# Two-layer hybrid encoder on one core: zero-padded score products, a corrected planning clock, a hand-written beginning, and one run of products with v per branch

## The chip, the core and the metric

The kernel runs on one core of a Trainium2 chip. A core has TensorE (matrix products, PE in the profile), VectorE (DVE), ScalarE (ACT), GpSimd (POOL) and SyncE (SP, which here only issues transfers), each with its own queue of instructions that it takes in order, and 16 DMA engines that move data between HBM and the core's memory. Products are written to PSUM, eight banks of 128 partitions by 512 fp32. The metric is the device time of one execution in microseconds; lower is better.

## What is computed

Two layers of an encoder on 256 tokens of width 1024. Cut to what matters:

```python
h = rms_norm(x, norm_mix_g); proj = h @ w_in                        # 9 blocks of 256 columns
ret  = retention(rq, rk, rv) ...    # 4 heads of 64: (q k^T * decay) v
na   = softmax(q k^T / 8 + bias) v  # 4 heads of 64, 256 tokens
mo   = softmax(q mk^T / 8) mv       # 4 heads of 64, 256 memory tokens
pool = window means of pv, a 64x64 map per group
up = einsum('bsnc,ncd->bsnd', stack([ret, pool, na, mo]), w_branch)
x = x + (sigmoid(h @ w_gate) * up).sum(n) @ w_out
a, g = split(rms_norm(x, norm_ffn_g) @ w_ffn_in); x = x + (silu(a) * g) @ w_ffn_out
```

All weights are fp32, 151 MB of them are read once.

## The kernel before

**Main products.** The 256 tokens are two tiles (t = 0, 1) of 128. The weights come as 276 slots of 128x1024 in the order in which they are used. A slot is loaded by SP into one of 4 buffers `raw`, copied by ACT to `whi` (rounded to fp32r, `split_hi`), and DVE writes the remainder `wlo = raw - whi` (`split_lo`). The activations are split the same way (`hhi`/`hlo` after a norm, `bhi`/`blo` after a branch), and a product of 128 tokens with 512 columns is three instructions on PE: hi by whi, hi by wlo, lo by whi (`emit`). There are 3312 of them, 96 of which are 256 columns wide, the rest 512.

**Small work.** Norms, head norms, transposes, scores, softmax, the products with v and the rest are generators ("chains") that run between the main products. `to_heads` turns q and k to heads with the tokens in the free dimension: `LS` holds the hi part of a head on 64 partitions and the lo part on the other 64, `RS` the hi part of the other operand on both halves. `scores` makes the scores of a head for 128 tokens in two products of 256 columns: LS (128 partitions) by RS, and the 64 partitions of the hi part in LS by `RL`, the lo part of the other operand. `attention` is called for branch 2 (neighbourhood) and branch 3 (memory), and works on two heads at a time (r = 0, 1): scores into the banks B, maximum, exp, scaling into `SC`, transposes back to B, a copy to `PT`, products with v into C[1]. The retention in `branch_chain` does the same with decays `DD` in place of a softmax.

**Order.** The program is written out instruction by instruction. What decides the order is a planning clock (`Clock`): each instruction that is given out is entered with an assumed cost, and a chain goes on when, by that clock, its operands should be there (`soon`, `there`, `need`, `background`). `pump` decides by the same clock when the next slot is split, and `ready` which tile's slot PE takes next. The clock has no part in the execution on the chip: there each engine runs its queue in order and waits on semaphores.

**Beginning.** x comes in four transfers of 128x512, all on SP's queue in turn with the identity (with the gains, `ident_gain`) and the first weight slots. `half_norm` turns and splits each half tile; products of zeros fill PE until the first operands are there.

Since a helper records every instruction for the clock, all instructions have the same line (L59); they are told apart by the names of their tiles: `A`, `B`, `C` are PSUM banks, `sc` and `pt` the softmax tiles, `qk` the values v (in the retention too), `w` scratch, `mem` the retention's decays.

Of the kernel before, what the change touches and what calls it, by code (L numbers as in the profile page):

```python
# [15 lines left out]
P = 128  # L16
D = 1024
KD = D // P
S = 256
# [16 lines left out]
WARM = 6.6  # L36
WINDOW = (6, 4, 1.5, 0.4)
# [5 lines left out]
class Engine:  # L43
    """An engine of nc whose instructions are also entered in the clock."""
# [4 lines left out]
    def __getattr__(self, op):  # L49
        f = getattr(self.real, op)  # L50

        def call(*args, **kw):
# [5 lines left out]
            self.clock.enter(self.name, op, outs, [v for v in ins + rest if isinstance(v, bass.AP)], kw)  # L58
# [5 lines left out]
class Clock:  # L64
    """An estimate in microseconds of when each engine gets to what has been given to it:
    the small work is handed out when its operands should be there, so that no queue waits on it."""
# [3 lines left out]
    def __init__(self):  # L70
        self.at = dict.fromkeys(("PE", "ACT", "DVE", "POOL", "SP", "DMA"), 0.6)
        self.reads, self.writes = {}, {}
        self.mark = 0.0
        self.column = None

# [4 lines left out]
    def cost(self, eng, op, outs, ins, kw):  # L80
        n = max([x.free_size() for x in outs[-1:] + ins[:1]])
        if eng == "PE":
            o = outs[0]
            n = o.free_size() * (2 if self.now < WARM else 1)
            if op == "transpose":
                return n * 0.84e-3
            if ins[0].dtype == F32R:
                return n * 0.416e-3 + 0.003
# [5 lines left out]
            return max(n, 128) * 1.67e-3  # L94
        if eng == "ACT":
            return 0.1 + n * 0.83e-3 + 0.1 * (kw.get("accum_out") is not None) + 0.04 * isinstance(kw.get("scale"), bass.AP)
        if eng == "POOL":
            return 0.3 + 0.17 * n
        if op in ("tensor_copy", "tensor_scalar", "tensor_scalar_mul", "tensor_scalar_add", "memset"):
            return 0.07 + n * 0.55e-3  # L100
        return 0.07 + n * 1.05e-3 + 0.05 * (op == "scalar_tensor_tensor")
# [18 lines left out]
    def enter(self, eng, op, outs, ins, kw):  # L120
# [5 lines left out]
                + [max(self.last(self.writes, x, skip), self.last(self.reads, x, skip)) + self.LATENCY for x in outs] + [self.at[eng]])  # L126
        if op == "dma_start":
            self.at[eng] = t + 0.48
            t = max(self.at["DMA"], t + 1.1) + (outs + ins)[0].nbytes() / 360e3
            self.at["DMA"] = t  # L130
            end = t + 0.9
# [16 lines left out]
def tile_encoder(ctx: ExitStack, tc: tile.TileContext, a: dict, out: bass.AP):  # L148
# [29 lines left out]
    RL = st([P, 2, S], F32R, "rl")  # L178
# [73 lines left out]
    state = {"dma": 0, "hi": 0, "lo": 0, "free": 0, "urgent": 0}  # L252
# [7 lines left out]
    def issue_dmas(n=NR):  # L260
        while state["dma"] < min(n_slots, state["lo"] + n):
# [3 lines left out]
            if len(dims) == 2:  # L265
# [6 lines left out]
    def split_hi():  # L272
        j = state["hi"]
        nc.scalar.copy(WHI[j % NS], RAW[j % NR])
        state["hi"] += 1
# [11 lines left out]
    def pump():  # L287
        """split weights when the engines have caught up, the sooner the fewer slots are ready"""
# [43 lines left out]
    def start(gen, *reads):  # L332
        """reads: PSUM banks that gen still reads, until it calls done()"""
# [3 lines left out]
    def until(step):  # L337
        """a chain goes on after what it has just given out (None), that much later (a number), or at a time"""
        return step[0] if isinstance(step, tuple) else clock.mark + (step or 0)

    def background():
        """let every chain go on whose last instructions should be through"""
# [39 lines left out]
    def scale_rows(out, in_, col):  # L382
        """out = in_ * col, on the engine that is free sooner"""
# [6 lines left out]
    def hi_lo(hi, lo, ps, bank, flag):  # L390
        """hi now, lo when hi is there, which ends the hold on bank"""
# [14 lines left out]
    def half_norm(src, t, c, act, gain, flag, bank, pre=None):  # L406
        """Half c of src (token-major) transposed, times gain (there a column), and split.
        What follows the products with it scales by one over the RMS (rms_chain)."""
# [22 lines left out]
    def rms_chain(src, rs, junk, flag, after=()):  # L431
        """rs = one over the RMS of each row of src"""
# [11 lines left out]
    def norm(t, flag, gain, rs, pre):  # L444
        """both halves of the norm of X[t]"""
# [7 lines left out]
    def head_norm(ps, dst, g, scale=None):  # L453
        """dst = ps (times scale, by row) scaled to unit RMS in groups of 64, g of them."""
# [662 lines left out]
```

## Time and profile before

| | before |
|---|---|
| time, median of 3 runs | 851.39 us (849.38 to 854.74) |
| profiled execution, first to last instruction | 850.4 us |
| PE busy | 840.0 us (99%) |
| DVE busy | 553.3 us (65%) |
| ACT busy | 469.6 us (55%) |
| POOL busy | 28.6 us (3%) |
| moved by DMA | 152.86 MB, 180 GB/s in the mean |

Busy time of PE overlaps: a product's own duration is longer than the step from one product to the next, so a PE that is shown as busy may still have waited some tenths of a microsecond. The step from one start to the next is what has to be read. In the rows below, times are in microseconds from the start of the span.

### The profile page before, as it was taken

To read this page: it belongs to the slowest core of one execution; us is meant where nothing else is said; L and a number is where in the kernel's file an instruction comes from. 1 tells how busy PE (TensorE), PEld (TensorE's weight loads), DVE (VectorE), ACT (ScalarE), POOL (GpSimd) and SP (SyncE) were. 2 spreads that over 40 slices of the span, in tenths; PEclk is the share of its full clock that TensorE was granted. 3 is DMA by queue.
4 is the path that set the end of the run, shared out by engine and by line. 5 is a ranking of instruction groups with operands and counts; after the bars stand their busy time and mean duration, and the time that the engine had idled before them with its cause. 6 is when DMAs were issued, how large, how long until landed. Compare 5 with 4: busy or idle time off the path is not lost.

```text
span 850.4 us, 10796 instructions
## 1 busy us (share of the span) xinstructions
PE 840.0 (99%) x3934; PEld 678.6 (80%) x3934; DVE 553.3 (65%) x807; ACT 469.6 (55%) x722; POOL 28.6 (3%) x30
## 2 busy tenths in 40 slices
PE   8999999999999999999999999999999999999998
PEld 7887777778887888888888877777788878888886
DVE  5898776665667656555568778567665775665541
ACT  7867867444556444444469676664454654444430
POOL 0300100000000000000012001000000000000000
PEclk9999999999999999999999999999999999999999
DMA  8946764454558666665363567345554675656611
GB/s 267 315 131 202 246 201 132 131 191 160 191 169 259 188 196 187 186 188 186 96 218 121 173 216 250 134 124 182 165 170 131 190 252 183 190 181 192 193 53 50
DMA packets 103749, 152.86 MB, mean 180 GB/s; under 512 B 6416, under 2 KB 55312, under 8 KB 103696
## 3 DMA queue, kind: packets, MB, share of 16 engines
q1 hardware_dynamic: 103696, 152.17, 56.3%
q8 instruction: 31, 0.51, 0.2%
q14 instruction: 22, 0.18, 0.1%
HBM read 151.10 MB, written 1.05 MB: 179 GB/s over the span
## 4 chain that ended last, share of the span: by engine, by line
PE 94%; DMA 3%; DVE 1%; ACT 1%; SPq 0%; issue 0%; DVEq 0%; ACTq 0%
PE A L59 62%; PE B L59 27%; PE C L59 5%; DMA raw<-in_w_ffn_out 2%; DMA mem<-in_pool_a 1%; DVE wlo L59 1%; DMA x<-in_x 1%; ACT whi L59 1%; DVE w L59 0%; SPq L59 0%; DVE x L59 0%; DVEq L1113 0%; ACTq L59 0%
## 5 line engine op out<-in xcount | busy, mean ns | idle before, releaser
L59 DVE TENSOR_TENSOR wlo<-raw,whi 128x1024 fp32r<-128x1024 f32 (+1 forms) x275 | 329.9, 1211 | 183.6 <-ACT whi L59 182.7
L59 ACT CAST whi<-raw 128x1024 fp32r<-128x1024 f32 x272 | 284.3, 1051 | 221.2 <-PE A L59 102.1
L59 PE MATMUL A<-whi,hhi 128*128 128x512 f32 (+1 forms) x544 | 215.6, 396 | 0.1
L59 PE MATMUL A<-whi,hlo 128*128 128x512 f32 (+1 forms) x544 | 209.4, 385 | 0.0
L59 PE MATMUL A<-wlo,hhi 128*128 128x512 f32 (+1 forms) x544 | 209.0, 384 | 0.0
L59 PEld LDWEIGHTS A<-whi,hhi 128*128 128x128 f32 x544 | 102.4, 188 | 24.1 <-issue 5.5
L59 PEld LDWEIGHTS A<-whi,hlo 128*128 128x128 f32 x544 | 102.4, 188 | 21.2 <-DVE hlo L59 0.5
L59 PEld LDWEIGHTS A<-wlo,hhi 128*128 128x128 f32 x544 | 102.6, 189 | 17.9
L59 PE MATMUL B<-whi,hlo 128*128 128x512 f32 x288 | 112.3, 390 | 0.1
L59 PE MATMUL B<-whi,hhi 128*128 128x512 f32 x288 | 112.3, 390 | 0.0
L59 PE MATMUL B<-wlo,hhi 128*128 128x512 f32 x288 | 112.1, 389 | 0.0
L59 PE MATMUL A<-whi,bhi 128*128 128x512 f32 x272 | 109.2, 401 | 0.0
L59 PE MATMUL A<-whi,blo 128*128 128x512 f32 x272 | 106.3, 391 | 0.0
L59 PE MATMUL A<-wlo,bhi 128*128 128x512 f32 x272 | 106.1, 390 | 0.0
L59 PEld LDWEIGHTS B<-whi,hlo 128*128 128x128 f32 x288 | 54.0, 188 | 12.1 <-DVE hlo L59 0.9
L59 PEld LDWEIGHTS B<-wlo,hhi 128*128 128x128 f32 x288 | 54.1, 188 | 11.2
L59 PEld LDWEIGHTS B<-whi,hhi 128*128 128x128 f32 x288 | 54.1, 188 | 11.1
L59 PEld LDWEIGHTS A<-whi,bhi 128*128 128x128 f32 x272 | 51.1, 188 | 11.4 <-issue 0.8
L59 PEld LDWEIGHTS A<-whi,blo 128*128 128x128 f32 x272 | 51.0, 188 | 11.0
L59 PEld LDWEIGHTS A<-wlo,bhi 128*128 128x128 f32 x272 | 51.2, 188 | 9.7
L59 DVE SCALAR_TENSOR_TENSOR w<-B,rms,w 128x256 f32<-128x256 f32 x72 | 34.6, 482 | 3.9 <-ACT w L59 2.6
L59 ACT CAST bhi<-C 128x512 fp32r<-128x512 f32 x28 | 16.4, 587 | 35.2 <-PE C L59 35.1
(112 smaller groups left out, 614.9 us busy)
## 6 DMA issues: line engine op xcount, KB each, us to landing
raw<-in_w_ffn_in SPq DMA_DIRECT2D x176, 256.0 KB, 3.3
raw<-in_w_gate SPq DMA_DIRECT2D x64, 512.0 KB, 3.8
raw<-in_w_ffn_out SPq DMA_DIRECT2D x44, 512.0 KB, 4.0
raw<-in_w_in SPq DMA_DIRECT2D x36, 512.0 KB, 4.6
raw<-in_w_branch SPq DMA_DIRECT2D x16, 512.0 KB, 5.0
raw<-in_w_out SPq DMA_DIRECT2D x16, 512.0 KB, 4.1
raw<-in_w_mem_kv SPq DMA_DIRECT2D x8, 512.0 KB, 5.1
xn<-in_bias SPq DMA_DIRECT2D x4, 512.0 KB, 5.8
```

Of the source, the lines that this page charges most:

```text
L59: return f(*args, **kw)
```

## The change

Four things are changed, and comments and descriptions are taken out.

1. `RL` gets a second half per head, so that it has the lo part of a head on the head's own 64 partitions and zeros (written once by GpSimd) on the other 64. The second product of `scores` now contracts over all 128 partitions.
2. In `attention` and in the retention the products with v of all four heads stand in one run behind the second pair of heads, in place of one run behind each pair. The second pair's turned probabilities go to `SC`, which the transposes have been read from, so that `PT` stays with the first pair.
3. The planning clock's prices are changed: a 512-wide product from 0.216 to 0.227 us, DVE and DMA by some per cent, 0.2 us where PE goes from a 64-partition fp32 product to another kind or back, and 1.28 us where ACT goes from exp to sigmoid or back.
4. The work up to slot 2 is written out in `begin` rather than planned: x's tile 0 is turned in two quarters, then the first slot's products for tile 0, then tile 1. The identity and tile 1's first half are loaded on ACT's queue, slot 0 in two transfers, copied and subtracted in halves. At the end each second store of a half block goes on ACT's queue.

```diff
...
 WARM = 6.6
+TABLE_LOAD = 1.28
...
                 outs.append(rest.pop(0))
-            self.clock.enter(self.name, op, outs, [v for v in ins + rest if isinstance(v, bass.AP)], kw)
+            func = next((v for v in rest if isinstance(v, AF)), None)
+            self.clock.enter(self.name, op, outs, [v for v in ins + rest if isinstance(v, bass.AP)], kw, func)
...
         self.column = None
+        self.narrow = False
+        self.table = None
...
             n = o.free_size() * (2 if self.now < WARM else 1)
+            narrow = op == "matmul" and ins[0].dtype == F32 and o.partition_size() == HD
+            change = 0.2 * (narrow != self.narrow)
+            self.narrow = narrow
             if op == "transpose":
-                return n * 0.84e-3
+                return n * 0.845e-3 + change
             if ins[0].dtype == F32R:
-                return n * 0.416e-3 + 0.003
+                return n * 0.4167e-3 + 0.0135 + change
...
                     return 0.02
-            return max(n, 128) * 1.67e-3
+            return max(n, 128) * 1.67e-3 + change
...
         if eng == "POOL":
+            if op == "memset":
+                return 0.1 + n * 1e-3
...
         if op in ("tensor_copy", "tensor_scalar", "tensor_scalar_mul", "tensor_scalar_add", "memset"):
-            return 0.07 + n * 0.55e-3
-        return 0.07 + n * 1.05e-3 + 0.05 * (op == "scalar_tensor_tensor")
+            return 0.085 + n * 0.6e-3
+        return 0.08 + n * 1.045e-3 + 0.05 * (op == "scalar_tensor_tensor")
...
-    def enter(self, eng, op, outs, ins, kw):
+    def enter(self, eng, op, outs, ins, kw, func=None):
...
                 + [max(self.last(self.writes, x, skip), self.last(self.reads, x, skip)) + self.LATENCY for x in outs] + [self.at[eng]])
+        if func in (AF.Exp, AF.Sigmoid) and func != self.table:
+            self.table = func
+            self.at["ACT"] += TABLE_LOAD
+            t = max(t, self.at["ACT"])
         if op == "dma_start":
-            self.at[eng] = t + 0.48
-            t = max(self.at["DMA"], t + 1.1) + (outs + ins)[0].nbytes() / 360e3
+            self.at[eng] = t + 0.45
+            t = max(self.at["DMA"], t + 1.2) + (outs + ins)[0].nbytes() / 390e3
             self.at["DMA"] = t
-            end = t + 0.9
+            end = t + 1.0
...
     RS = st([P, 2, 2, S], F32R, "rs")
-    RL = st([P, 2, S], F32R, "rl")
+    RL = st([P, 2, 2, S], F32R, "rl")
...
     HALVES = [slice(c * 512, (c + 1) * 512) for c in range(2)]
-    state = {"dma": 0, "hi": 0, "lo": 0, "free": 0, "urgent": 0}
+    state = {"dma": 0, "hi": 0, "lo": 0, "free": 0, "urgent": 0, "by_hand": False}
...
             dst = shaped(RAW[j % NR], dims)
-            if len(dims) == 2:
+            if len(dims) == 2 and j:
...
         j = state["hi"]
-        nc.scalar.copy(WHI[j % NS], RAW[j % NR])
+        for o in HALVES if j < 1 else [slice(None)]:
+            nc.scalar.copy(WHI[j % NS][:, o], RAW[j % NR][:, o])
...
+        if state["by_hand"]:
+            return
...
         for i in range(2):
-            lo(RL[own[i]], C[1], gains[1], i, RS[own[i], i])
+            lo(RL[own[i], i], C[1], gains[1], i, RS[own[i], i])
...
         r, i = h // 2, h % 2
-        own = slice(i * HD, (i + 1) * HD)
         nc.tensor.matmul(out, LS[:, i, r, tok], RS[:, i, r, :], start=True, stop=False)
-        nc.tensor.matmul(out, LS[own, i, r, tok], RL[own, r, :], start=False, stop=True)
+        nc.tensor.matmul(out, LS[:, i, r, tok], RL[:, i, r, :], start=False, stop=True)
...
+        turned = [PT, SC]
...
                         nc.tensor.transpose(half(B[i])[:, m, t * P:(t + 1) * P], half(SC[i])[:, t, m * P:(m + 1) * P], ident)
-                nc.scalar.copy(PT[i], B[i])
+                nc.scalar.copy(turned[r][i], B[i])
...
             yield
+        for r in range(2):
...
                     h = 2 * r + i
-                    nc.tensor.matmul(half(C[1])[i * HD:(i + 1) * HD, r, :], half(v)[:, m, h * HD:(h + 1) * HD], half(PT[i])[:, m, :],
+                    nc.tensor.matmul(half(C[1])[i * HD:(i + 1) * HD, r, :], half(v)[:, m, h * HD:(h + 1) * HD], half(turned[r][i])[:, m, :],
                                      start=(m == 0), stop=(m == 1), skip_group_check=True)
-            yield
+        yield
...
         yield
-        for r in range(6):
-            if r < 4:
-                ps = B[r % 2]
-                for m in range(2):
-                    scores(half(ps)[:, m, :], r, slice(m * P, (m + 1) * P))
-                nc.vector.scalar_tensor_tensor(out=DD[r], in0=ps, scalar=HD ** -0.5, in1=DD[r], op0=ALU.mult, op1=ALU.mult)
+        for r in range(4):
+            ps = B[r % 2]
+            for m in range(2):
+                scores(half(ps)[:, m, :], r, slice(m * P, (m + 1) * P))
+            nc.vector.scalar_tensor_tensor(out=DD[r], in0=ps, scalar=HD ** -0.5, in1=DD[r], op0=ALU.mult, op1=ALU.mult)
...
                 nc.vector.tensor_tensor(out=half(gs), in0=half(gs), in1=rgb.unsqueeze(1).to_broadcast([P, NT, BW]), op=ALU.mult)
-            if 2 <= r:
-                h = r - 2
-                if h % 2:
-                    for m in range(2):
-                        for i in range(2):
-                            nc.tensor.matmul(half(C[1])[i * HD:(i + 1) * HD, h // 2, :], half(rv)[:, m, (h - 1 + i) * HD:(h + i) * HD],
-                                             half(DD[h - 1 + i])[:, m, :], start=(m == 0), stop=(m == 1), skip_group_check=True)
-                    nc.scalar.copy(half(W[4])[:, h // 2, :], half(C[1])[:, h // 2, :])
-            yield
+            yield
+        for r in range(2):
+            for m in range(2):
+                for i in range(2):
+                    h = 2 * r + i
+                    nc.tensor.matmul(half(C[1])[i * HD:(i + 1) * HD, r, :], half(rv)[:, m, h * HD:(h + 1) * HD], half(DD[h])[:, m, :],
+                                     start=(m == 0), stop=(m == 1), skip_group_check=True)
+        nc.scalar.copy(W[4], C[1])
+        yield
...
-        t0, t1, t2 = (st([P, 16], F32, f"ls{i}") for i in range(3))
...
+        t0, t1, t2 = (rgb[:, 16 * i:16 * i + 16] for i in range(3))
...
     def store(t, blk):
-        for c in range(blk * 512, blk * 512 + 512, 256):
+        for i, c in enumerate(range(blk * 512, blk * 512 + 512, 256)):
...
             nc.vector.tensor_add(o, o, A[2 * t + blk][:, c % 512:c % 512 + 256])
-            nc.sync.dma_start(out=out[0, t * P:(t + 1) * P, c:c + 256], in_=o)
+            (nc.scalar if i else nc.sync).dma_start(out=out[0, t * P:(t + 1) * P, c:c + 256], in_=o)
...
-    def warm(*aps):
...
-        while clock.now < max(clock.last(clock.writes, x) for x in aps):
-            nc.tensor.matmul(B[0][:, 0:P], W[0][:, 0:P], W[0][:, P:2 * P], start=True, stop=True)
-            clock.at["PE"] += 0.21 if clock.now < 6.2 else 0
+    def warm(n):
...
+        for _ in range(n):
+            nc.tensor.matmul(B[0][:, 0:P], W[0][:, 0:P], W[0][:, 0:P], start=True, stop=True)
...
+    def begin():
...
+        parts = {(0, 0): (C[0], (0, 1)), (0, 1): (B[1], (2, 3)), (1, 0): (C[1], (0, 1)), (1, 1): (A[3], (2, 3)),
+                 (0, 2): (C[0], (4, 5, 6, 7)), (1, 2): (C[1], (4, 5, 6, 7))}
...
+        def turn(t, *which):
+            for c in which:
+                bank, ks = parts[t, c]
+                for i, k in enumerate(ks):
+                    nc.tensor.transpose(bank[:, i * P:(i + 1) * P], X[t][:, k * P:(k + 1) * P], ident)
...
+        def split(t, c):
+            bank, ks = parts[t, c]
+            ks = [(bank[:, i * P:(i + 1) * P], GAIN[0][0][:, k:k + 1], *act_h(t, k)) for i, k in enumerate(ks)]
+            for ps, g, hi, lo in ks:
+                nc.scalar.activation(hi, ps, AF.Copy, scale=g)
+            for ps, g, hi, lo in ks:
+                nc.vector.scalar_tensor_tensor(out=lo, in0=ps, scalar=g, in1=hi.bitcast(F32), op0=ALU.mult, op1=ALU.subtract)
+            if c:
+                raise_flag(f"h{t}@0c{c - 1}")
...
+        def weights():
+            split_hi()
+            split_lo()
...
+        state["by_hand"] = True
+        warm(6)
+        turn(0, 0, 1)
+        warm(2)
+        split(0, 0)
+        weights()
+        emit(0)
+        turn(1, 0, 1)
+        split(0, 1)
+        split(1, 0)
+        emit(1)
+        weights()
+        split(1, 1)
+        turn(0, 2)
+        emit(0)
+        turn(1, 2)
+        split(0, 2)
+        weights()
+        emit(1)
+        split(1, 2)
+        weights()
+        emit(0)
+        emit(1)
+        state["by_hand"] = False
...
     def first_rms(t):
-        while state["hi"] < 3 + t:
+        while state["hi"] < 5 + t:
...
         nc.vector.memset(mhalf, -0.5)
-        def load_x(t, c):
-            nc.sync.dma_start(out=X[t][:, HALVES[c]], in_=a["x"][0, t * P:(t + 1) * P, HALVES[c]])
...
+        for i in range(2):
+            nc.gpsimd.memset(RL[(1 - i) * HD:(2 - i) * HD, i].bitcast(F32), 0.0)
+        def load_x(queue, t, c):
+            queue.dma_start(out=X[t][:, HALVES[c]], in_=a["x"][0, t * P:(t + 1) * P, HALVES[c]])
...
+        nc.scalar.dma_start(out=ident_gain, in_=a["ident_gain"])
+        load_x(nc.sync, 0, 0)
...
         clock.at["ACT"] += 1.2
-        load_x(0, 0)
-        nc.sync.dma_start(out=ident_gain, in_=a["ident_gain"])
-        issue_dmas(1)
-        load_x(1, 0)
+        load_x(nc.scalar, 1, 0)
         issue_dmas(2)
-        load_x(0, 1)
-        load_x(1, 1)
+        load_x(nc.sync, 0, 1)
+        issue_dmas(3)
+        load_x(nc.sync, 1, 1)
         issue_dmas()
-        for c in range(2):
-            for t in range(NT):
-                start(half_norm(X[t], t, c, act_h, GAIN[0][0], f"h{t}@0", (C[0], B[1], C[1], A[3])[2 * t + c]))
...
         assert base[0] == n_slots
+        begin()
...
             else:
-                if pos[0] == 0:
-                    nc.tensor.matmul(B[0][:, 0:P], W[0][:, 0:P], W[0][:, 0:P], start=True, stop=True)
-                    continue
...
```

The order of the built programs shows it at three places, all on PE. The beginning before (`w0` holds zeros, `x0`, `x1` are the tiles of x, `hhi0`, `hlo0` tile 0's split activations):

```order
L59 MATMUL C0_67<-ident_gain_131,x0_105 128x128
L59 MATMUL C0_67<-ident_gain_131,x0_105 128x128 x3
L59 MATMUL B0_65<-w0_125 128x128 x3
L59 MATMUL C1_68<-ident_gain_131,x1_106 128x128
L59 MATMUL C1_68<-ident_gain_131,x1_106 128x128 x3
L59 MATMUL B0_65<-w0_125 128x128 x2
L59 MATMUL A0_61<-whi0_73,hhi0_93 128x512
L59 MATMUL A0_61<-wlo0_83,hhi0_93 128x512
L59 MATMUL A0_61<-whi0_73,hlo0_95 128x512
L59 MATMUL B1_66<-ident_gain_131,x0_105 128x128
```

and now:

```order
L61 MATMUL B1_66<-ident_gain_131,x0_105 128x128 x2
L61 MATMUL B0_65<-w0_125 128x128 x2
L61 MATMUL A0_61<-whi0_73,hhi0_93 128x512
L61 MATMUL A0_61<-wlo0_83,hhi0_93 128x512
L61 MATMUL A0_61<-whi0_73,hlo0_95 128x512
L61 MATMUL A0_61<-whi0_73,hhi0_93 128x512
L61 MATMUL A0_61<-wlo0_83,hhi0_93 128x512
L61 MATMUL A0_61<-whi0_73,hlo0_95 128x512
L61 MATMUL C1_68<-ident_gain_131,x1_106 128x128
L61 MATMUL C1_68<-ident_gain_131,x1_106 128x128
L61 MATMUL A3_64<-ident_gain_131,x1_106 128x128 x2
```

The transposes of tile 1 have moved from ahead of the first main product to behind the sixth; on SP's queue slot 0 has moved up by one place, and tile 1's first half no longer stands between slots 0 and 1.

The transposes of the FFN's second hidden block in layer 0 (`w2`, `w3` hold tile 1's silu(a) * g), whose inputs follow the last product into A2, which stands 12 rows ahead of the first row here, before:

```order
L59 MATMUL A1_62<-whi9_82,hhi0_93 128x512
L59 MATMUL A1_62<-wlo9_92,hhi0_93 128x512
L59 MATMUL A1_62<-whi9_82,hlo0_95 128x512
L59 MATMUL A1_62<-whi9_82,hhi0_93 128x512
L59 MATMUL A1_62<-wlo9_92,hhi0_93 128x512
L59 MATMUL A1_62<-whi9_82,hlo0_95 128x512
L59 MATMUL C1_68<-ident_gain_131,w2_127 128x128
```

and now, with the same 12 rows ahead:

```order
L61 MATMUL A1_62<-whi9_82,hhi0_93 128x512
L61 MATMUL A1_62<-wlo9_92,hhi0_93 128x512
L61 MATMUL A1_62<-whi9_82,hlo0_95 128x512
L61 MATMUL C1_68<-ident_gain_131,w2_127 128x128
L61 MATMUL C1_68<-ident_gain_131,w3_128 128x128
```

18 main products stood between the block's last product and its transposes, and 15 stand there now. Layer 1 has the same shift.

The products with v of branch 2 in layer 0, first pair of heads, before:

```order
L59 MATMUL A3_64<-whi8_81,hlo1_96 128x512
L59 MATMUL C1_68<-pt0_121,qk0_111 64x256
L59 MATMUL C1_68<-pt1_122,qk0_111 64x256
L59 MATMUL C1_68<-pt0_121,qk0_111 64x256
L59 MATMUL C1_68<-pt1_122,qk0_111 64x256
L59 MATMUL A1_62<-whi9_82,hhi0_93 128x512
```

and now, behind the second pair, both pairs in one run:

```order
L61 MATMUL A0_61<-whi4_77,bhi2_99 128x512
L61 MATMUL A0_61<-wlo4_87,bhi2_99 128x512
L61 MATMUL A0_61<-whi4_77,blo2_103 128x512
L61 MATMUL C1_68<-pt0_121,qk0_111 64x256
L61 MATMUL C1_68<-pt1_122,qk0_111 64x256
L61 MATMUL C1_68<-pt0_121,qk0_111 64x256
L61 MATMUL C1_68<-pt1_122,qk0_111 64x256
L61 MATMUL C1_68<-sc0_119,qk0_111 64x256
L61 MATMUL C1_68<-sc1_120,qk0_111 64x256
L61 MATMUL C1_68<-sc0_119,qk0_111 64x256
L61 MATMUL C1_68<-sc1_120,qk0_111 64x256
L61 MATMUL A0_61<-whi4_77,bhi2_99 128x512
```

The run behind the first pair is gone, and the one behind the second pair is twice as long. Over the program twelve such runs become six. The number of main products (3312), transposes (344) and score products (96) stays.

## Rows read from the trace of the kernel before

**Rows 1.** The page: busy time, share of the span and instructions of each engine.

```profile
PE 840.0 (99%) x3934; PEld 678.6 (80%) x3934; DVE 553.3 (65%) x807; ACT 469.6 (55%) x722; POOL 28.6 (3%) x30
```

**Rows 2.** Waits of PE: who for whom, us in total, times, longest.

```profile
PE C L59 <- DVE w L59: 2.8, 4, 1.1
```

**Rows 3.** Timeline of PE, last products: start us, us, engine line op, tiles, shape.

```profile
844.12 0.39 PE L59 MATMUL A<-whi,blo 128*128 128x512 f32 x1
...
846.16 0.39 PE L59 MATMUL A<-whi,blo 128*128 128x512 f32 x1
```

**Rows 4.** Groups of PE by shape: count, busy us, mean ns, idle before.

```profile
L59 PE MATMUL B<-rl,ls 64*128 64x256 f32 x48 | 18.3, 381 | 0.0
L59 PE MATMUL B<-rs,ls 128*128 128x256 f32 x48 | 16.7, 349 | 0.0
...
L59 PE MATMUL C<-pt,qk 128*64 128x256 f32 x64 | 8.7, 392 | 0.0
...
L59 PE MATMUL C<-mem,qk 128*64 128x256 f32 x32 | 4.3, 392 | 0.0
```

**Rows 5.** Timeline of PE, a block of eight score products.

```profile
71.40 0.28 PE L59 MATMUL B<-rs,ls 128*128 128x256 f32 x1
71.61 0.38 PE L59 MATMUL B<-rl,ls 64*128 64x256 f32 x1
71.92 0.39 PE L59 MATMUL B<-rs,ls 128*128 128x256 f32 x1
...
73.80 0.50 PE L59 MATMUL A<-whi,hhi 128*128 128x512 f32 x1
74.14 0.40 PE L59 MATMUL A<-wlo,hhi 128*128 128x512 f32 x1
```

**Rows 6.** Timeline of PE, first and last of 36 main products 256 wide.

```profile
60.10 0.28 PE L59 MATMUL A<-whi,hhi 128*128 128x256 f32 x1
...
64.29 0.28 PE L59 MATMUL A<-whi,hlo 128*128 128x256 f32 x1
```

**Rows 7.** Timeline of PE around a run of products with v.

```profile
69.27 0.39 PE L59 MATMUL A<-whi,hlo 128*128 128x512 f32 x1
69.58 1.08 PE L59 MATMUL C<-pt,qk 128*64 128x256 f32 x8
70.60 0.50 PE L59 MATMUL A<-whi,hhi 128*128 128x512 f32 x1
70.93 0.39 PE L59 MATMUL A<-wlo,hhi 128*128 128x512 f32 x1
```

**Rows 8.** Timeline of all engines, the beginning; in brackets idle before and what ended it.

```profile
6.17 1.04 ACT L59 CAST whi<-raw 128x1024 fp32r<-128x1024 f32 x1 [0.30 <-DMA raw<-in_w_in]
...
7.25 1.29 DVE L59 TENSOR_TENSOR wlo<-raw,whi 128x512 fp32r<-128x512 f32 x2 [0.22 <-ACT whi L59]
...
7.80 1.12 PE L59 MATMUL C<-ident_gain,x 128*128 128x128 f32 x4 [2.44 <-DMA x<-in_x]
...
9.42 0.77 PE L59 MATMUL A<-whi,hhi 128*128 128x512 f32 x1
...
12.49 0.48 PE L59 MATMUL A<-whi,hhi 128*128 128x512 f32 x1
```

**Rows 9.** Stretches of the beginning, PE: busy us (instructions), granted clock, DMA share, GB/s.

```profile
4.40:7.70 3.30, 0.96 (x9) 1.00 0.95 311
7.80:11.10 3.30, 3.30 (x13) 0.50 1.05 403
```

**Rows 10.** Timeline, a softmax of the memory attention, layer 1: scaling, then its transposes.

```profile
536.52 0.52 ACT L59 ACTIVATE sc<-sc,sums 128x256 f32<-128x256 f32 x1
...
537.28 0.60 PE L59 MATMUL B<-ident_gain,sc 128*128 128x128 f32 x4
```

**Rows 11.** Timeline of PE, transposes of the FFN's second hidden block, layer 0.

```profile
269.10 0.33 PE L59 MATMUL C<-ident_gain,w 128*128 128x128 f32 x1 [1.05 <-DVE w L59]
```

**Rows 12.** Timeline of DVE, the last additions of the residual ahead of the stores.

```profile
846.59 0.75 DVE L59 TENSOR_TENSOR x<-x,A 128x256 f32<-128x256 f32 x2 [0.61 <-PE A L59]
```

## The prediction

> **What bounds the kernel now.** I read the busy times first: PE is busy for 840.0 of 850.4 us and the next engine, DVE, for 553.3 [rows 1]. A busy PE may still wait inside its products, so I looked at PE's waits next. They are few: its longest entry towards DVE is 2.8 us in four waits [rows 2]. So the time is the sum of PE's steps from one start to the next, and a change of this kernel is worth what it does to those steps, or to the stretch at the beginning in which PE has no operands. The rest of the reading is therefore about steps. A plain main product takes (846.16 − 844.12)/9 = 0.227 us [rows 3], one of 256 columns (64.29 − 60.10)/35 = 0.120 [rows 6]. All steps that differ from these are the small work, and I went through them kind by kind.
>
> **Zeros in RL.** Per [rows 4] there are 48 score products over 128 rows (rs, ls) and 48 over 64 rows (rl, ls). A block of eight shows them in turn [rows 5]: the first step is 71.61 − 71.40 = 0.21, and the other seven take (73.80 − 71.61)/7 = 0.313 each, so the block takes 2.40. Even the main product behind it steps by 74.14 − 73.80 = 0.34 in place of 0.227. Both kinds are 256 columns wide, and full-height products of that width step by 0.120 where they stand among themselves [rows 6]; so what costs is the alternation of 128 and 64 rows. With zeros in the other half every score product has the full height. I take 0.120 for each of them and 0.227 for the main product behind. A block of eight then saves 2.40 + 0.34 − 0.96 − 0.227 = 1.55. The 96 products stand in eight blocks of eight (retention, per two heads) and eight of four. A block of four takes 0.21 + 3 × 0.313 + 0.34 now and 0.48 + 0.227 then, which saves 0.775. Sum: 8 × 1.55 + 8 × 0.775 = **−18.6**. The bounds: if a padded product were still at the 0.21 of a block's first step, the saving would be 96 × 0.09 = 8.6 less, −10.0; more than −18.6 has no row for it. I take 0.120, because LS is a 128-row operand in both products, and rows 6 shows full height, full width of stationary and the same 256 columns. The memset of zeros runs on POOL, which is busy for 28.6 of 850.4 us [rows 1]; without that cover it would cost PE nothing before the first score product.
>
> The row shows a 64-row product at a step of 0.313 and no two of them side by side. The Trainium skill, "TensorEngine Tiling (Array Packing)", sections Key Properties and Performance Considerations, says that a change of tiling mode drains TensorE, which agrees with the 0.313, and that contractions up to 64 should be tiled by rows for up to twice the speed, which speaks against padding. By the first sentence the sum stays at −18.6; by the second a 64-row product is worth half a full one, 0.06, and the padding adds 48 × 0.06 = 2.9, an estimate from that page.
>
> **Products with v.** The 64 + 32 rows of [rows 4] are twelve runs of eight rows. A run costs more than its products at both ends [rows 7]: the step into it is 69.58 − 69.27 = 0.31, 0.08 over a plain one, and the first main product behind it steps by 70.93 − 70.60 = 0.33, 0.10 over. The change leaves six longer runs with the same products. Each run that goes saves at least 0.18, and at most 0.18 + 0.31, if its last product too has a step of a change between kinds such as 0.313 in [rows 5]. Between 0.18 and 0.49 I take 0.30: 6 × 0.30 = **−1.8** (−1.1 to −2.9). The first pair's products now come later, but nothing waits for them alone: the copy out of C[1] already followed the second pair's. The retention's copies become one of 512 columns on ACT, which is busy for 55% [rows 1].
>
> **Beginning.** ACT copies slot 0 at 6.17 for 1.04, DVE makes the remainder from 7.25, and PE's transposes of tile 1 wait 2.44 for x until 7.80 [rows 8]. Main products begin at 9.42 and run without a hole from 12.49, when six are done. In the new order tile 1's transposes stand behind six products of tile 0, so the first product needs only slot 0's first half: 6.17 + 0.52 (half of 1.04) = 6.69. With half a remainder per 0.65 (1.29 for two) the products of slot 0 follow to about 8.5. I expect 12 to 18 products by 12.5 in place of six: 6 to 12 steps of 0.227, 1.4 to 2.7; **−2.0**. The granted clock bounds it: it was 1.00 from 4.40 to 7.70, in which PE was busy for 0.96 of 3.30, and 0.50 behind that, from 7.80 to 11.10 [rows 9]. If the twelve products all stand at 0.50 they cost 0.227 each more, 2.7, and the term is +0.7. If the clock is higher there, and the beginning gives all twelve, it is −3. The transfers bound it too: at the 403 GB/s of [rows 9] the 512 KB of a slot take 1.3, and nothing in the change makes them less, so tile 1 cannot run much ahead of 9.
>
> The Trainium skill, "DMA: Bandwidth & Descriptors", section "Issuing engines are not separate DMA queues", says that transfers from any engine's queue run on the same 16 DMA engines and interleave. By it the identity and tile 1's half on ACT's queue save time of issue and no time of transfer; the DMA share of 0.95 to 1.05 in [rows 9] fits, and the term is unchanged.
>
> **Planning clock.** The chip does not use it; what changes is how many main products stand between a producer and its transposes on PE. The order has eight softmax stages of the memory attention and of the neighbourhood in which that distance changes: by +1, +3, +3 and −6 products in layer 0, and by −7, −9, −6 and −3 in layer 1, each of 0.227. Distance costs nothing where slack was left. It is short at the stage of [rows 10]: the scaling ends at 536.52 + 0.52 = 537.04 and the transposes start at 537.28, so 0.24 is spare, and six products less, 1.36, leave a wait of **+1.1**. The others had a slack of about 1 or more, or gained distance. The FFN's second hidden block stands three products closer (18 to 15), and its transposes wait 1.05 already [rows 11], so 0.68 more is waited, in both layers: **+1.4**. Together **+2.5**. From below: −2, if ACT and DVE get to these chains earlier by as much (2.8 is all that could go [rows 2]). From above: +7, if four of the stages that came closer wait as long as the worst.
>
> **End.** The last additions stand on DVE behind the last products [rows 12], as before, and the store behind them has to wait for them on either queue: 0.
>
> **Sum.** 850.4 − 18.6 − 1.8 − 2.0 + 2.5 = 830.5 for the profiled execution. The median of the runs shown is 851.39, 1.0 above the profiled one, so I forecast **831.5**.
>
> **Rivals.**
> *The padded product does not get the step of a full one.* Then the change doesn't do what it says: 850.4 − 1.8 − 2.0 + 2.5 = 849.1, with the 1.0 about 850. For it: LS is used as stationary in pairs, and a new stationary has to be loaded for each. Against it: main products of 256 columns change stationary as well and step by 0.120 [rows 6].
> *The closer distances cost more.* With the bound of +7 and up to 5 more where layer 1's stages lose 6 to 9 products: 836 to 843. For it: one stage had a slack of 0.24 [rows 10]. Against it: the waits of all before are 2.8 [rows 2].
> *The start gives all and the waits do not come.* 850.4 − 18.6 − 2.9 − 3 − 2 + 1.0 = 825, so 823 to 827.
> *Slower.* The corrected clock may plan the splitting of a slot later, so that PE stands at the remainder's product. The place is the second product of each slot; with 276 slots less the four at the start it takes 20.4 + 4.8 = 25.2 us, 0.09 a slot, to be 1% slower than before. For it: DVE's remainder takes 1.29 of a slot [rows 8]. Against it: a slot has twelve products, 2.7 us, and DVE is busy for 65% [rows 1]. It would give 855 to 865. By the row-tiling rule named above, padding takes 48 × 0.06 = 2.9 more where I count 18.6 less, and the time would be 850.4 + 2.9 − 1.8 − 2.0 + 2.5 = 852; [rows 5], with 0.313 a step, doesn't bear it out.
>
> **How the numbers follow.** The forecast, 827 to 836, has 0.75; the start in full 0.06; closer distances 0.12; no gain from padding 0.05, the row-tiling rule in it; slower 0.02. The range from 826.5 to 837.0 takes in the forecast with the bounds of v (−1.1 to −2.9), the beginning (−3 to +0.7) and part of the clock's, and leaves out what lies above and below. About 1% is what a measurement of this kernel can tell from no change: 842.9 to 859.9. Faster by more: 0.75 + 0.06 + 0.11 = 0.92; within: 0.01 + 0.05 = 0.06; slower: 0.02.
>
> **What would show it.** Steps between rs and rl at 0.12, none at 0.31, and a plain step behind a block. Six runs of 16 rows with v. A first main product near 6.7 and more than twelve by 12.5; if the granted clock stays at 0.50 to 11, the beginning gave little. PE's waits for DVE and ACT near 5 in all; if they are over 10, the clock term was wrong. If the steps of padded products stay near 0.2 or above, the first term is wrong, and with it the forecast.

## The result, and the profile after

The changed kernel takes 844.46 us (median of 5 runs, 841.89 to 845.22) against 851.28 for the kernel before (849.38 to 854.74); the ratio is 0.9907, 95% interval 0.9883 to 0.9930. That is 0.9% faster, where 831.5 (2.3%) was forecast, with a range from 826.5 to 837.0: the direction holds, the size does not. The profiled execution takes 840.0 us, 10.4 less than that of before. The page's first line and the three longest of PE's waits (who for whom, us in total, times, longest):

```profile
PE 820.8 (98%) x3928; PEld 672.4 (80%) x3928; DVE 552.2 (66%) x802; ACT 470.1 (56%) x726; POOL 30.5 (4%) x32
...
PE C L61 <- DVE w L61: 7.6, 5, 3.0
PE C L61 <- DVE blo L61: 1.8, 2, 1.6
PE B L61 <- DMA mem<-in_pool_a: 1.8, 3, 1.1
```

PE is busy for 19.2 us less than in [rows 1], close to the 19.9 by which the forecast shortens the span, but the span is only 10.4 shorter. The difference stands in the waits: the line of [rows 2] has grown from 2.8 to 7.6 us, and others have come, of which the two longest are shown. All of PE's entries add up to 6.3 us before and to 15.0 after.

The scores (PE's timeline, a block of eight; compare [rows 5]):

```profile
69.66 0.28 PE L61 MATMUL B<-rs,ls 128*128 128x256 f32 x1
69.77 0.28 PE L61 MATMUL B<-rl,ls 128*128 128x256 f32 x1
69.89 0.28 PE L61 MATMUL B<-rs,ls 128*128 128x256 f32 x1
...
70.61 0.40 PE L61 MATMUL A<-whi,hhi 128*128 128x512 f32 x1
70.85 0.40 PE L61 MATMUL A<-wlo,hhi 128*128 128x512 f32 x1
```

Every step is 0.12, the block takes 0.95 where it took 2.40, and the product behind it steps by 0.24 in place of 0.34. The same timeline around a run of products with v (compare [rows 7]):

```profile
131.30 0.40 PE L61 MATMUL A<-whi,hlo 128*128 128x512 f32 x1
131.63 1.08 PE L61 MATMUL C<-pt,qk 128*64 128x256 f32 x8
132.54 1.03 PE L61 MATMUL C<-sc,qk 128*64 128x256 f32 x8
133.51 0.50 PE L61 MATMUL A<-whi,hhi 128*128 128x512 f32 x1
133.84 0.40 PE L61 MATMUL A<-wlo,hhi 128*128 128x512 f32 x1
```

The long run takes 1.88 where two took 1.02 each, and there is one entry and one exit less. The beginning (first product of tile 0, first of tile 1; then stretches of PE: busy us, granted clock as a share of the full one, DMA share, GB/s; compare [rows 8, 9]):

```profile
6.38 0.49 PE L61 MATMUL A<-whi,hhi 128*128 128x512 f32 x1 [0.71 <-ACT whi L61]
...
9.90 0.50 PE L61 MATMUL A<-whi,hhi 128*128 128x512 f32 x1 [0.24 <-ACT hhi L61]
```

```profile
4.40:7.70 3.30, 2.36 (x11) 1.00 0.97 333
7.80:11.10 3.30, 2.83 (x12) 1.00 1.05 400
```

The first product is 3.0 us earlier, and the granted clock is 1.00 in both stretches, where it was 0.50, the lower of its two levels (1.2 of 2.4 GHz), from 7.80 to 11.10.

### The profile page after: what moved, and what is told of

Its sections match the earlier page's. It is cut to its first block, busy times and chain, and to the rows that moved or that the text cites. A ratio compares the mean times of both kernels' runs of the same rounds, so it can differ in the third digit from the quotient of the medians.

```text
span 840.0 us, 10795 instructions
## 1 busy us (share of the span) xinstructions
PE 820.8 (98%) x3928; PEld 672.4 (80%) x3928; DVE 552.2 (66%) x802; ACT 470.1 (56%) x726; POOL 30.5 (4%) x32
## 3 DMA queue, kind: packets, MB, share of 16 engines
HBM read 151.10 MB, written 1.05 MB: 181 GB/s over the span
## 4 chain that ended last, share of the span: by engine, by line
PE 78%; ACT 7%; DMA 7%; DVE 6%; issue 2%; POOL 0%; SPq 0%; DVEq 0%; ACTq 0%; POOLq 0%
PE A L61 49%; PE B L61 25%; PE C L61 4%; DVE wlo L61 3%; ACT whi L61 2%; DMA raw<-in_w_in 2%; DMA mem<-in_pool_a 2%; DMA raw<-in_w_ffn_out 1%; DMA raw<-in_w_gate 1%; DVE w L61 1%; ACT rs L61 1%; ACT sc L61 1%; DMA raw<-in_w_mem_kv 1%; ACT qk L61 1%; ACT bhi L61 1%
## 5 line engine op out<-in xcount | busy, mean ns | idle before, releaser
L61 ACT CAST whi<-raw 128x1024 fp32r<-128x1024 f32 (+1 forms) x273 | 284.1, 1050 | 214.0 <-PE A L61 83.0
L61 PEld LDWEIGHTS B<-whi,hlo 128*128 128x128 f32 x288 | 54.0, 188 | 12.9 <-DVE hlo L61 1.8
L61 PEld LDWEIGHTS A<-whi,bhi 128*128 128x128 f32 x272 | 51.1, 188 | 10.4 <-issue 0.8
```

The lines of the kernel that those rows point to most:

```text
L61: return f(*args, **kw)
```

## Where the time went

In layer 1, the transposes of `w` to heads (PE) with the steps before them; in brackets the idle time before and what ended it:

```profile
505.56 1.05 ACT L61 CAST whi<-raw 128x1024 fp32r<-128x1024 f32 x1 [1.63 <-PE A L61]
...
506.88 0.47 ACT L61 ACTIVATE w<-A,rms 128x256 f32<-128x256 f32 x1
...
509.02 0.49 ACT L61 ACTIVATE w<-A,rms 128x256 f32<-128x256 f32 x1
...
511.03 0.71 PE L61 MATMUL C<-ident_gain,w 128*128 128x128 f32 x5
511.15 0.41 DVE L61 TENSOR_REDUCE sm<-w 128x4 f32<-128x256 f32 x1
...
511.93 1.86 POOL L61 TENSOR_TENSOR sm<-sm,mhalf 128x4 f32<-128x4 f32 x1 [1.50 <-DVE sm L61]
...
513.83 0.23 DVE L61 TENSOR_SCALAR sm<-sm,rms 128x4 f32<-128x4 f32 x1 [0.90 <-POOL sm L61]
514.16 0.42 DVE L61 TENSOR_TENSOR w<-A,sm 128x256 f32<-128x256 f32 x1
...
514.73 0.52 PE L61 MATMUL C<-ident_gain,w 128*128 128x128 f32 x3 [2.99 <-DVE w L61]
```

and the same steps before:

```profile
514.78 0.49 ACT L59 ACTIVATE w<-A,rms 128x256 f32<-128x256 f32 x1
...
518.81 0.71 PE L59 MATMUL C<-ident_gain,w 128*128 128x128 f32 x5
...
520.04 0.52 PE L59 MATMUL C<-ident_gain,w 128*128 128x128 f32 x3 [0.52 <-DVE w L59]
```

The transposes stand as many main products (24) behind the end of w's block as before. But on ACT a slot's copy now stands ahead of the copy to `w` and waits 1.63 for a buffer that PE still reads, so the second `w` comes 511.03 − 509.02 = 2.0 ahead of the transposes where it came 4.0 ahead. Reduction, power on POOL (1.86) and scaling then follow while PE waits. Counting main products between a producer and PE, as the prediction did, misses this: two other queues lie between. In layer 0 the same transposes even stand behind 27 main products in place of 24, and PE waits twice, where before it waited once, for 0.52:

```profile
100.08 0.30 PE L61 MATMUL C<-ident_gain,w 128*128 128x128 f32 x1 [1.32 <-DVE w L61]
101.07 0.52 PE L61 MATMUL C<-ident_gain,w 128*128 128x128 f32 x3 [0.69 <-DVE w L61]
```

To compare whole kernels I added up, from PE's timelines behind the 12th main product, whatever a step takes beyond the usual one of its pair of products where that is over 0.15 us: 4.4 us before, 14.9 after, good to some tenths. The table below uses this sum. It also takes in steps that are longer because the granted clock was low: none in the three kernels before, padding alone and changed, but up to some 4 us in others.

## The experiments

Theory P: the new prices of the planning clock place the work so that waits take the gain back. Theory L: PE has less work to cover the small work with, so it waits whatever the plan. The first four kernels tell them apart: the first and third have exactly the orders of before and of after (but for two memsets on POOL), the second and fourth change the prices alone.

**Padding alone:** before, with part 1 of the change.

> The kernel before with the zero-padded score products alone; each engine's instructions stand in the order of before. Theory P (prices: the new price table of the planning clock hands the transposes to PE too early, and some 11 us of the gain come back as waits there): nothing is given back here, so the score steps fall to 0.12 and the whole 18.3 us come off: span about 832, PE's waits for DVE about as before (2.8 us). Theory L (less PE time: small work is as late as before whatever the prices are, so waits take back what the scores save): span about 840, with 8 to 11 us of new waits at the head transposes.

833.04 us, ratio to before 0.9791 (95% interval 0.9767 to 0.9816), profiled 831.9. This is P, and not L: nothing is given back. All of PE's waits:

```profile
PE C L59 <- DVE w L59: 2.7, 4, 0.9
PE C L59 <- DMA x<-in_x: 2.0, 1, 2.0
PE B L59 <- DVE mhalf L59: 1.0, 1, 1.0
PE B L59 <- DMA mem<-in_pool_a: 0.3, 1, 0.3
```

PE's waits for `w` are those of [rows 2] to 0.1 us, although PE arrives 18 us earlier at the end.

**Old prices:** the changed kernel with `cost` and `enter` of before.

> The changed kernel with the prices of the planning clock before (padding, one run of products with v, and the beginning by hand stay). Theory P: the waits at the head transposes go, span about 829 to 832. Theory L: span about 840, waits as in the changed kernel.

837.03, ratio 0.9847 (0.9817 to 0.9877). Between the two: half of the loss goes, but 5 us stay that padding alone doesn't have.

**No padding:** after, with

```diff
-        nc.tensor.matmul(out, LS[:, i, r, tok], RL[:, i, r, :], start=False, stop=True)
+        nc.tensor.matmul(out, LS[i * HD:(i + 1) * HD, i, r, tok], RL[i * HD:(i + 1) * HD, r, :], start=False, stop=True)
```

and `RL` without its zeros, as before.

> The changed kernel with RL and the second score product over 64 rows as before; each engine's instructions stand in the order of the changed kernel. Theory P: the scores cost their 18.3 us again and the waits stay, span about 858. Theory L: the longer scores cover the waits, so only some 8 us come back, span about 848.

856.63, ratio 1.0077 (1.0043 to 1.0111), which is slower than before. By the ratios padding is worth 1.0077 − 0.9907 = 0.0170 in this order (14.5 us) and 0.0209 (17.8) in that of before; the longer scores cover at most some 3 us of the waits, no more than the intervals leave open. In the two profiled executions PE's waits add up to 11.4 us here and to 15.0 with padding, which fits. So it is P, with at most a small part of L.

**New prices alone:** before, with part 3 of the change.

> The kernel before with the new prices of the planning clock alone. Theory P: some 10 us slower than before, span about 860, with PE waiting for DVE at the head transposes. Theory L: span 849 to 852, since the long score steps still cover the small work.

860.85, ratio 1.0121 (1.0100 to 1.0143): 10 us lost, as P said. Part 3 by itself makes the kernel slower.

Next, which price it is, and what the two other parts bring alone.

**Old price of a main product**, in the changed kernel:

```diff
-                return n * 0.4167e-3 + 0.0135 + change
+                return n * 0.416e-3 + 0.003 + change
```

The price of a transpose goes back with it (`0.845e-3` to `0.84e-3`).

> The changed kernel with the old prices of a main product (0.216 us for 512 columns in place of 0.227) and of a transpose alone; the rest of the new prices stays. Theory P1 (PE's price takes the spare away: priced right, PE gets the transposes as soon as the clock thinks their inputs done, with nothing left for what the clock still has too low): recovers most of the 7.4 us that the old prices as a whole recover, about 836 to 839. Theory P2 (the DMA prices and the table load): stays at about 844.

838.88, ratio 0.9846 (0.9826 to 0.9865): some 5 us come back, as P1 (PE's price) said.

**Old prices of transfers, no table load:** `0.45`, `1.2`, `390e3`, `1.0` and `TABLE_LOAD` back to `0.48`, `1.1`, `360e3`, `0.9` and 0.

> The changed kernel with the old prices of transfers and no price for a table load; PE's and DVE's new prices stay. Theory P1: stays at about 844. Theory P2: recovers most of the 7.4 us, about 836 to 839.

844.90, ratio 0.9926 (0.9895 to 0.9956): nothing comes back, so it is not P2 (transfers and table load).

**Padding and one run with v**, old prices and beginning.

> Padding with the old prices and the old beginning, and the products with v in one run. By the steps at a run's ends 0.30 us for each of six runs: 1.8 less than padding alone, about 831.2. If the longer chain of a branch delays what follows: 833 or more.

835.07, ratio 0.9814 (0.9780 to 0.9848), within the intervals of padding alone. The 1.8 us don't show in the time; 4.5 us more by the sum over steps take their place (1.3 of them at the lower granted clock).

**Padding and the beginning by hand**, old prices.

> Padding with the old prices and the beginning by hand. The changed kernel's trace reaches its 36th main product 1.45 us earlier than before with the same small work left, so 831.6 if the rest keeps its waits. If the other beginning shifts the plan of what follows so that waits come: 833 or more; the kernel with the old prices, 4 us slower than padding alone, says that this run or the one with v must lose.

840.79, ratio 0.9862 (0.9845 to 0.9878): 6 us slower than padding alone, by waits far behind the beginning (one of 3.2, from 99 us on).

Theory Q then named one price that is plainly wrong in both tables: a power of 4 columns on POOL counts 0.98 and took 1.01 to 2.04.

**The power priced as measured**, in the changed kernel (`return 0.6 if n == 1 else 1.9`), then in padding alone, then in the changed kernel with the old price of a main product (and of a transpose):

> The changed kernel with POOL's power priced as the traces show it (1.9 us for 4 or 8 columns in place of 0.98 and 1.66, 0.6 for one in place of 0.47). Theory Q (the head transposes wait because the clock counts 0.9 us too little for the power in the head norms' chain, which the old, too low price of a main product did not cover by itself but lengthened in products): the waits of the head transposes fall from 7.6 to about 3 us, time about 839. Theory R (the waits come from slot copies that stand ahead of the chain's steps on ACT and DVE, and the price of the power is not what decides): stays within 2 us of 844.

842.35, ratio 0.9903 (0.9888 to 0.9918).

> Padding with the old prices and the old beginning, and POOL's power priced as the traces show it. Theory Q: the head transposes' waits of 2.7 us go, 831. Theory R: 833 or above, since a new order brings new waits elsewhere.

841.26, ratio 0.9890 (0.9856 to 0.9925).

> The changed kernel with the old price of a main product and POOL's power as the traces show it. Theory Q: below the 838.9 of the old price of a main product alone by 2 to 4 us, about 835 to 837. Theory R: 839 or above.

837.63, ratio 0.9852 (0.9810 to 0.9894).

**Transposes to heads handed out 1.2 us later** (`yield 1.2` at the head of `to_heads`):

> The changed kernel, in which the transposes to heads go to PE 1.2 us later than the clock finds their inputs done, and nothing else. Theory Q: the 7.6 us of waits for w fall by 1.2 for each of the head transposes that wait now, to some 4, time about 840. Theory R: the same, if the chain itself is not moved; if the time stays at 844, the waits of the head transposes were not what the new prices cost.

846.41, ratio 0.9950 (0.9924 to 0.9976). PE's two longest waits:

```profile
PE C L61 <- DVE w L61: 5.6, 5, 1.7
PE A L61 <- ACT gt L61: 4.2, 1, 4.2
```

The waits for `w` fall from 7.6 to 5.6, and a new one of 4.2 comes elsewhere. Q falls: a truer price of the power gains nothing, and costs 8 us on the good plan.

So I asked whether it is prices at all. Theory S: any other order than that of before costs 4 to 13 us. Two fixed costs were moved by 5 ns (`0.1` to `0.105` for ACT, `0.07` to `0.075` for DVE), and two new prices were put in alone, all with padding and the old beginning.

> Padding with the old prices and the old beginning; the clock's fixed cost of an ACT instruction is 0.105 in place of 0.100 us, which is enough to give another order. Theory P (particular prices cause the waits): within 2 us of padding alone, about 833. Theory S (the order before was an unusually good one for the chip, and another order costs 4 to 13 us whatever led to it): 837 to 846.

842.52, ratio 0.9898 (0.9873 to 0.9923).

> Padding with the old prices and the old beginning; the clock's fixed cost of the dearer DVE instructions is 0.075 in place of 0.070 us. Theory P: about 833. Theory S: 837 to 846.

838.25, ratio 0.9860 (0.9834 to 0.9887).

> Padding with the old beginning and the old prices but for the main product, 0.227 in place of 0.216. Theory P: 838 to 841, the 5 us that the old price of a main product recovered in the changed kernel. Theory S: 837 to 846, no more and no less than with 5 ns on another price.

844.12, ratio 0.9916 (0.9890 to 0.9942).

> Padding with the old beginning and the old prices but for DVE's, which are the new ones. Theory P: 833 to 835. Theory S: 837 to 846.

837.17, ratio 0.9843 (0.9823 to 0.9863).

5 ns on a price, which say nothing of the chip, cost 9 us on ACT's and 6 on DVE's. ACT and PE of the kernel with 5 ns on ACT, where its longest wait is:

```profile
104.09 2.77 ACT L59 ACTIVATE rs<-C,cols 64x512 fp32r<-64x512 f32 x4
106.88 1.28 ACT L59 ACT_TABLE_LOAD   x1
108.17 1.27 ACT L59 ACTIVATE gt<-A,rms 128x512 f32<-128x512 f32 x2
```

```profile
106.22 0.39 PE L59 MATMUL A<-whi,blo 128*128 128x512 f32 x1
108.91 0.50 PE L59 MATMUL A<-whi,bhi 128*128 128x512 f32 x1 [2.30 <-ACT gt L59]
```

PE waits for the bank that the gate's sigmoid still reads; on ACT four copies to RS and a table load stand ahead of that sigmoid. Again the queue of another engine, not a distance on PE.

Yet the five padded kernels with the new, higher price of a main product had the highest ratios of the padded ones, though the nearest pair (0.9903 and 0.9898) can't be told apart. Theory M: a price below the true 0.227 is a margin, since a chain's next step goes to PE when the clock thinks its inputs done. The last two kernels count 0.205 (`n * 0.395e-3 + 0.003`): padding alone, and the changed kernel.

> Padding with the old beginning and the old prices but for the main product, which the clock counts at 0.205 us for 512 columns (0.216 before, 0.227 the true step). Theory M (a low price is a margin: the lower, the fewer waits): 833 to 837, below the replanned kernels with 0.216. Theory S (chance among orders): anywhere from 837 to 846.

837.40, ratio 0.9850 (0.9822 to 0.9878).

> The changed kernel with a main product at 0.205 us in the clock, all other new prices kept. Theory M: below the 838.9 that 0.216 gave, 833 to 837. Theory S: 837 to 846, on either side of it.

832.88, ratio 0.9786 (0.9771 to 0.9800), profiled 831.1. It beats both kernels, and equals padding alone. Its longest waits:

```profile
PE A L61 <- ACT bhi L61: 1.9, 1, 1.9
PE B L61 <- DVE mhalf L61: 1.0, 1, 1.0
PE A L61 <- DVE blo L61: 0.8, 1, 0.8
PE C L61 <- ACT sc L61: 0.6, 1, 0.6
```

`w` has no line any more. In layer 1 its transposes stand behind 27 main products, four other transposes and the run with v, where the changed kernel has 24 main products alone. ACT's second copy to `w` comes 6.9 ahead of them in place of 2.0:

```profile
496.50 0.49 ACT L61 ACTIVATE w<-A,rms 128x256 f32<-128x256 f32 x1
...
503.36 1.03 PE L61 MATMUL C<-ident_gain,w 128*128 128x128 f32 x8
```

M fits the changed kernel, whose three prices stand in order (0.9786, 0.9846, 0.9907), though the middle one also has the old price of a transpose; on padding alone 0.205 is 5 us worse than the plan of before, as S has it. S as it was put falls here too: this is another order, and it costs next to nothing.

| kernel | price of a main product | ratio to before | longer steps, sum in us |
|---|---|---|---|
| before | 0.216 | 1 | 4.4 |
| padding alone | 0.216 | 0.9791 | 4.6 |
| changed, 0.205 | 0.205 | 0.9786 | 5.5 |
| padding, 0.205 | 0.205 | 0.9850 | 8.2 |
| nine other padded plans | 0.216 | 0.9814 to 0.9898 | 8.6 to 13.9 |
| changed kernel | 0.227 | 0.9907 | 14.9 |
| four other padded plans | 0.227 | 0.9903 to 0.9950 | 14.3 to 21.3 |

## Why the prediction was wrong, step by step

**Zeros in RL** (−18.6): right. A block of eight saves 2.40 + 0.34 − 0.95 − 0.24 = 1.55 as worked out, and padding alone gives 17.8 in the medians. The Trainium skill, "TensorEngine Tiling (Array Packing)", sections Theoretical Speedup and When to Use Tiling, has contractions up to 64 tiled by rows for up to twice the speed, from which the prediction estimated that padding would cost 2.9. The traces don't bear that estimate out here: the 64-row products stepped by 0.31, the padded ones by 0.12.

**Products with v** (−1.8): right by the steps. Two runs of 1.02 with 0.08 and 0.10 at their ends make 2.40, the long run 1.88 + 0.10 + 0.10 = 2.08; that is 0.32 for each of six, 1.9. In the time of a kernel of its own it can't be seen, because the order changes with it.

**Beginning** (−2.0): the mechanism was right and the size wrong. The first product came at 6.38 (6.69 forecast), fifteen products were given out by 12.5, and against the profiled execution of before the 36th product is 1.45 earlier. But over all traces that gain doesn't show: in ten with the old beginning the 36th product stands at 17.5 to 20.5, 18.3 in the mean, and in ten with the beginning by hand at 17.7 to 19.1, 18.3 in the mean. The granted clock moves it by more: three of the ten by hand have a stretch at 0.50 within the first 13 us and stand at 19.0 to 19.1, the other seven at 17.7 to 18.5. The term's worth is about nothing.

**Planning clock** (+2.5, −2 to +7): this is the step that failed. Waits rose by 14.9 − 4.4 = 10.5; by the prediction's own sign, PE's entries towards DVE and ACT, which should have been near 5, add up to 12.9. Of its two entries, the FFN's second block was right in layer 0: 15 products in place of 18, and a longer wait.

```profile
263.01 0.55 PE L61 MATMUL C<-ident_gain,w 128*128 128x128 f32 x3 [1.68 <-DVE w L61]
```

That is 0.63 more than the 1.05 of [rows 11], where 0.68 was forecast; in layer 1 it was about 0.2 more. The stage of [rows 10] got no wait at all. The largest waits came where the prediction didn't look, at the transposes to heads, the longest at an unchanged distance on PE and that at 100 us at a greater one. I read the slack before from one good order and moved only PE's rows; the slack itself depends on where slot copies, table loads and reductions stand on ACT and DVE, and these were replanned too. The term should have been the price of a new plan: 4 to 17 us more by the sum over steps in the fourteen other padded plans with 0.216 or 0.227. The rival of closer distances (836 to 843) came nearest in time, but distance is not what made the longest waits.

**End** (0): right. From the start of the last product to the end of the span it is 4.2 us in both.

**Sum.** −18.6 − 1.9 − 1.45 + 10.5 = −11.45, against −10.4 of the two profiled executions; 1 us is left over and was not traced. Three slips in the prediction's working change none of this: the blocks of eight scores are the attention's and those of four the retention's; with its bounds, closer distances give 836 to 841; and the rival of a slower kernel needs 20.4 + 8.5 = 28.9 us, 0.11 a slot, to be 1% above before.

What stays open: why the order of before is so good, and how much of the effect of the main product's price is margin and how much chance. The first four kernels show that new orders, and not the shorter scores, take the gain back, and that about half of it goes by the prices; which price does it is not shown, since 5 ns on another one move as much. M was shown on one kernel at three prices, and padding alone at 0.216 stands outside its series.

## What to carry to other kernels

Where a planner writes the order, an edit to its prices or to anything it plans is first of all a new order: time a step of 5 ns on a price to learn what a new order costs, and price that, not the steps that the diff names. A correct price can cost time: part 3 alone lost 10 us. That the error in it had been a margin for what the planner leaves out fits the runs and is not shown. An edit that leaves every queue's order alone, such as the zeros here, can be predicted from its steps: 18.6 was forecast, and it gave 17.8 in one order and 14.5 in another.

## What the runs showed of the hardware

Alternating products of 128 and 64 rows, 256 columns wide, cost 0.31 a step where full ones cost 0.12: 64 more rows of zeros are free, and save 0.19 on each product of a pair. No run has two such 64-row products side by side, so it stays open whether the alternation costs or the 64 rows themselves.

A wait can cost more than itself. In the kernel with 5 ns on ACT the granted clock (third number from the right) falls to its lower level, 0.50, behind the 2.30 of wait; the rows give means over their stretches:

```profile
106.20:110.90 4.70, 2.40 (x14) 0.95 0.57 183
110.90:114.20 3.30, 3.30 (x10) 0.56 0.43 136
```

Steps of main products there are 0.2 longer, 1.4 us for seven of them. Thirteen of the twenty traces have such stretches between the beginning and the last 20 us; those of before, padding alone and the changed kernel have none. In the changed kernel's profiled execution the 2.99 had no such sequel:

```profile
511.00:515.00 4.00, 1.01 (x9) 1.00 0.63 198
515.00:518.00 3.00, 3.00 (x16) 1.00 0.60 176
```
